# Hybrid decoder step on one core: the three partial products of a pair of k-tiles in another order

## The chip, the cores and the metric

One launch of the kernel runs on one NeuronCore of a Trainium2 chip. The metric is the device time of one execution in microseconds; the number given for a kernel is the median of several executions. All inputs and outputs lie in HBM. TensorE multiplies a stationary operand (the weights of a matmul, loaded by an instruction of its own, LDWEIGHTS) with a moving operand and adds the product into PSUM.

## The reference, cut to what matters

The layer takes 256 prompt tokens and 8 x 4 sample tokens, together 288 rows, through one decoder layer in float32. Nearly all of its arithmetic is products of these 288 rows with large weight matrices:

```
xn = rmsnorm(x, norm_mix)
z, xbc, dt, q, k, v, r, g, gate_a, gate_b = split(xn @ w_in)      # 2048 x 15408
branch_a = ssd(z, xbc, dt) @ w_ssd_out                            # 2048 x 2048
branch_b = gla(q, k, v, r, g) @ w_gla_out
h = x + (sigmoid(gate_a) * branch_a + sigmoid(gate_b) * branch_b) @ w_mix_out
h = h + cross_attend(rmsnorm(h) @ w_cq, mem_k, mem_v) @ w_co
up = causal_conv(rmsnorm(h) @ w_up)                               # 2048 x 11264
h = h + (silu(up[gate half]) * up[other half]) @ w_down           # 5632 x 2048
```

`mem_k` and `mem_v` of the prompt are `rmsnorm(mem) @ w_ck` and `@ w_cv`. The state updates of the convolutions, the SSD scan and the GLA scan are outputs too.

## The kernel before, in words

Every float32 operand of a projection is split into two halves, hi (the value rounded to the type in which TensorE takes it, `F32R`) and lo (the rest, rounded likewise). A product W·x is taken as three products, hi·hi, hi·lo and lo·hi, all added into the same PSUM accumulator.

The activations are kept transposed, channels on the 128 partitions and the 288 tokens in the free dimension, so a weight tile of 128 x 128 is the stationary operand and 128 x 288 of activations move. All projections but those of the memory go through `proj_w` (lines 114 to 138), called by `proj` with a matrix and a block of (mostly) 256 of its columns. It takes `nt` accumulators of 128 output channels (two for 256 columns; the narrow projection of `dt` has one), and walks down the contraction dimension:

- `wload` (lines 102 to 105) has SP's queue load four k-tiles of 128 x 256 into a tile `raw`, of which there are `RB` = 3.
- For each pair of k-tiles `wsplit` (lines 94 to 100) makes `whi` with a cast on ScalarE (line 97) and `wlo` = `raw` - `whi` with a subtraction on VectorE (line 99). There are `WB` = 5 buffers of each; a cast can be written only when the matmuls that read the buffer's former content are done.
- For each of the two accumulators j the six matmuls of the pair follow: line 129 is hi·hi and line 130 hi·lo, for k = 0 and then k = 1; line 133 is lo·hi for k = 0 and k = 1. So lines 129 and 130 load the same 128 x 128 weights one directly after the other. I call these six matmuls a group; two groups make a pair's twelve.
- After the last pair `cons` reads the accumulator. Four accumulators (`acc`) rotate.

The projections of the memory (`mem_proj`, lines 287 to 322) have the roles exchanged: activations are the stationary operand, 512 columns of weights move, and the order of lines 313, 314 and 317 is hi·hi, lo·hi for each of two accumulators, then hi·lo for both. They don't change. Nor do the small products of the attention, lines 1346 to 1348 and 1387 to 1389, which have the same three-product form.

`weave` runs the steps of a background part (the scans, the attention) between the steps of a projection. The framework orders the instructions of each engine when the program is built: it takes them in the order written where it holds their inputs for ready by then, and lets a later instruction pass where it doesn't. On the chip each engine's order is fixed and semaphores do the waiting. Matmuls that add into one accumulator keep their order.

Of the kernel before, what the change touches and what calls it, by code (L numbers as in the profile page):

```python
# [40 lines left out]
def hybrid_step(ctx: ExitStack, tc: tile.TileContext, I: dict, O: list):  # L41
# [3 lines left out]
    MM, TR = nc.tensor.matmul, nc.tensor.transpose  # L45
# [10 lines left out]
    def acc_tile():  # L56
        return ps.tile([P, 512], F32, tag="acc", bufs=4, name="acc")

    def mm_tile():
        return ps.tile([P, 512], F32, tag="mm", bufs=3, name="mm")  # L60
# [33 lines left out]
    def wsplit(raw):  # L94

        hi = wp.tile(list(raw.shape), F32R, tag="whi", bufs=WB, name="whi")
        S.copy(hi, raw)  # L97
        lo = wp.tile(list(raw.shape), F32R, tag="wlo", bufs=WB, name="wlo")
        V.tensor_tensor(lo, raw, hi, ALU.subtract)  # L99
        return hi, lo  # L100
# [8 lines left out]
    def flush():  # L109

        while late:
            late.pop(0)()

    def proj_w(load, ncol, X, nk, cons, N=T):

        nt = (ncol + P - 1) // P
        accs = [acc_tile() for _ in range(nt)]
        for k0 in range(0, nk, 4):
            kn = min(4, nk - k0)
            raw = load(k0, kn)  # L120
            for s0 in range(0, kn, 2):
                hi, lo = wsplit(raw[:, s0:s0 + 2, :])
                for j in range(nt):
                    m = min(P, ncol - j * P)
                    a = accs[j][0:m, 0:N]
                    cs = slice(j * P, j * P + m)
                    for k in range(2):
                        xh, xl = X(k0 + s0 + k)
                        MM(a, hi[:, k, cs], xh, start=(k0 + s0 + k == 0), stop=False)  # L129
                        MM(a, hi[:, k, cs], xl, start=False, stop=False)  # L130
                    for k in range(2):
                        xh, xl = X(k0 + s0 + k)
                        MM(a, lo[:, k, cs], xh, start=False, stop=(k0 + s0 + k == nk - 1))  # L133
                    if k0 + s0 + 2 == nk:
                        cons(j, a)
                if k0 + s0 == min(4, nk - 2):
                    flush()
                yield

    def proj(w, c0, ncol, X, nk, cons, row0=0):  # L140
        def load(k0, kn):
            return wload(w[row0 + k0 * P:row0 + (k0 + kn) * P, c0:c0 + ncol].rearrange("(k p) n -> p k n", p=P))
        return proj_w(load, ncol, X, nk, cons)
# [40 lines left out]
    def halves(alloc, name):  # L184

        ts = [alloc(f"{name}{i}") for i in range(2)]

        def at(k, n=None):
            t, o = ts[k // 8], k % 8
            if n is None:  # L190
                return t[:, o, :], t[:, 8 + o, :]
            return t[:, o:o + n, :], t[:, 8 + o:8 + o + n, :]
        return at
# [55 lines left out]
    X = halves(bigr, "xn")  # L249
    with pool("p0") as p0:  # L250
# [207 lines left out]
        def dt_cons(j, a):  # L458
# [4 lines left out]
            V.tensor_tensor(lr3[64:80, :], a[64:80], lr3[64:80, :], ALU.subtract)  # L463

        run(proj_w(dt_load, 112, X, KT, dt_cons))

        def dt_prep():
# [682 lines left out]
    for n in range(8):  # L1150
        kind, i = units[n]
# [66 lines left out]
    for j2 in range(KT // 2):  # L1218
        def cons(j, a, j2=j2):
            added(hx[j2][:, j, :], 2 * j2 + j, a, vec("norm_cross"), hn, acc)  # L1220
# [198 lines left out]
    a = mm_tile()  # L1419
# [143 lines left out]
    a = acc_tile()  # L1563
# [61 lines left out]
```

## Time and profile before

| | us |
|---|---|
| median of 3 runs (lowest to highest) | 2608.87 (2606.83 to 2610.24) |
| the profiled execution | 2607.92 |
| its span, first to last instruction | 2606.2 |
| TensorE matmul busy | 2576.2 (99%) |
| TensorE weight load busy | 2473.3 (95%) |
| VectorE, ScalarE, GpSimd busy | 1718.2, 1376.2, 308.2 |
| mean granted TensorE clock, as a share of full speed | 0.996 |

Weight loads stand in the profile on a row of their own (PEld) beside the matmuls (PE). Matmuls are pipelined: the duration of one covers parts of its neighbours, so the pace of a chain is read from the difference of the starts of successive matmuls. The profile names a matmul by its line, by the tiles it reads (`acc<-mx,whi`: activations `mx`, weights `whi`), and by the shapes of the stationary and the moving operand (128\*128, 128x288).

### The profile page before, as it was taken

To read this page: it belongs to the slowest core of one execution; us is meant where nothing else is said; L and a number is where in the kernel's file an instruction comes from. 1 tells how busy PE (TensorE), PEld (TensorE's weight loads), DVE (VectorE), ACT (ScalarE), POOL (GpSimd) and SP (SyncE) were. 2 spreads that over 40 slices of the span, in tenths; PEclk is the share of its full clock that TensorE was granted. 3 is DMA by queue.
4 is the path that set the end of the run, shared out by engine and by line. 5 is a ranking of instruction groups with operands and counts; after the bars stand their busy time and mean duration, and the time that the engine had idled before them with its cause. 6 is when DMAs were issued, how large, how long until landed. Compare 5 with 4: busy or idle time off the path is not lost. (4 is left out here: it accounts for less than half of the span.)

```text
span 2606.2 us, 50491 instructions
## 1 busy us (share of the span) xinstructions
PE 2576.2 (99%) x19123; PEld 2473.3 (95%) x19123; DVE 1718.2 (66%) x3683; ACT 1376.2 (53%) x2796; POOL 308.2 (12%) x425
## 2 busy tenths in 40 slices
PE   8999999999999999999999999999999999999998
PEld 7889999999989998999999989899999999999998
DVE  5655786886766566666666555567777677675765
ACT  7655655564645463534455544455545454454545
POOL 2003021100000000000000222202202020110200
PEclk9999999999999999999999999999999999999999
DMA  7666566665676666777666778655555555555553
GB/s 250 208 225 205 179 200 179 201 195 148 201 234 212 199 213 218 225 233 237 182 207 214 246 262 298 213 166 168 166 170 166 168 161 172 168 160 178 164 171 126
DMA packets 435280, 514.07 MB, mean 197 GB/s; under 512 B 23208, under 2 KB 384984, under 8 KB 434716
## 3 DMA queue, kind: packets, MB, share of 16 engines
q1 hardware_dynamic: 408684, 423.16, 52.5%
q0 software_dynamic: 26320, 87.68, 10.1%
q8 instruction: 150, 2.46, 0.4%
q14 instruction: 94, 0.77, 0.1%
q10 hardware_dynamic: 32, 0.01, 0.0%
HBM read 465.27 MB, written 45.48 MB: 196 GB/s over the span
## 5 line engine op out<-in xcount | busy, mean ns | idle before, releaser
L99 DVE TENSOR_TENSOR wlo<-raw,whi 128x512 fp32r<-128x512 f32 (+1 forms) x1464 | 989.5, 689 | 703.3 <-ACT whi L97 689.6
L97 ACT CAST whi<-raw 128x512 fp32r<-128x512 f32 (+1 forms) x1464 | 898.2, 618 | 1043.8 <-PE acc L130 824.1
L129 PE MATMUL acc<-xn,whi 128*128 128x288 f32 (+1 forms) x1936 | 551.0, 300 | 2.8 <-ACT whi L97 2.8
L130 PE MATMUL acc<-xn,whi 128*128 128x288 f32 (+1 forms) x1936 | 542.5, 295 | 0.0
L133 PE MATMUL acc<-xn,wlo 128*128 128x288 f32 (+1 forms) x1936 | 413.0, 295 | 1.4 <-DVE wlo L99 1.4
L129 PE MATMUL acc<-hf,whi 128*128 128x288 f32 x1408 | 396.0, 296 | 0.0
L130 PE MATMUL acc<-hf,whi 128*128 128x288 f32 x1408 | 393.5, 295 | 0.0
L129 PEld LDWEIGHTS acc<-xn,whi 128*128 128x128 f32 (+1 forms) x1936 | 365.0, 189 | 10.2 <-issue 6.7
L130 PEld LDWEIGHTS acc<-xn,whi 128*128 128x128 f32 (+1 forms) x1936 | 365.2, 189 | 4.2 <-issue 1.0
L133 PEld LDWEIGHTS acc<-xn,wlo 128*128 128x128 f32 (+1 forms) x1936 | 311.3, 188 | 1.8 <-DVE wlo L99 1.7
L133 PE MATMUL acc<-hf,wlo 128*128 128x288 f32 x1408 | 302.2, 296 | 0.0
L130 PEld LDWEIGHTS acc<-hf,whi 128*128 128x128 f32 x1408 | 265.1, 188 | 0.1
L129 PEld LDWEIGHTS acc<-hf,whi 128*128 128x128 f32 x1408 | 264.7, 188 | 0.1
L133 PEld LDWEIGHTS acc<-hf,wlo 128*128 128x128 f32 x1408 | 225.4, 188 | 0.0
L130 PE MATMUL acc<-pr,whi 128*128 128x288 f32 x704 | 196.6, 295 | 0.0
L129 PE MATMUL acc<-pr,whi 128*128 128x288 f32 x704 | 195.9, 294 | 0.0
L129 PE MATMUL acc<-un,whi 128*128 128x288 f32 x512 | 153.3, 315 | 2.3 <-DVE mb L897 1.0
L133 PE MATMUL acc<-pr,wlo 128*128 128x288 f32 x704 | 147.8, 291 | 0.0
L1457 POOL COPY fsp<-fst 128x16 f32<-128x16 f32 x88 | 105.4, 1222 | 335.3 <-ACT fcg L1463 87.8
L130 PE MATMUL acc<-un,whi 128*128 128x288 f32 x512 | 143.2, 295 | 0.0
L130 PEld LDWEIGHTS acc<-pr,whi 128*128 128x128 f32 x704 | 132.4, 188 | 0.0
L129 PEld LDWEIGHTS acc<-pr,whi 128*128 128x128 f32 x704 | 132.1, 188 | 0.0
(525 smaller groups left out, 4245.3 us busy)
## 6 DMA issues: line engine op xcount, KB each, us to landing
raw<-in_w_in_dram SPq DMA_DIRECT2D x240, 512.0 KB
raw<-in_w_up_dram SPq DMA_DIRECT2D x176, 512.0 KB
raw<-in_w_down_dram SPq DMA_DIRECT2D x88, 512.0 KB
raw<-in_w_ck_dram SPq DMA_DIRECT2D x32, 512.0 KB
raw<-in_w_cv_dram SPq DMA_DIRECT2D x32, 512.0 KB
raw<-in_w_ssd_out_dram SPq DMA_DIRECT2D x32, 512.0 KB
sin<-in_state_gla_dram POOLq DMA_DIRECT2D x32, 512.0 KB, 5.7
out_dram<-sin SPq DMA_DIRECT2D x32, 512.0 KB
```

Of the source, the lines that this page charges most:

```text
L97: S.copy(hi, raw)
L99: V.tensor_tensor(lo, raw, hi, ALU.subtract)
L129: MM(a, hi[:, k, cs], xh, start=(k0 + s0 + k == 0), stop=False)
L130: MM(a, hi[:, k, cs], xl, start=False, stop=False)
L133: MM(a, lo[:, k, cs], xh, start=False, stop=(k0 + s0 + k == nk - 1))
L1457: G.tensor_copy(sp[:, :, 0:2], st.rearrange("p (b k) -> p b k", k=2))
```

## The change

The six matmuls of a group are written in another order: first hi·hi for k = 0 and 1, then lo·hi for k = 0 and 1, then hi·lo for k = 0 and 1. In the weights they load, the order was hi0 hi0 hi1 hi1 lo0 lo1 and is hi0 hi1 lo0 lo1 hi0 hi1; in the activations they move, it was h0 l0 h1 l1 h0 h1 and is h0 h1 h0 h1 l0 l1. The start flag stays on the group's first matmul, and the stop flag is now on the last hi·lo. Nothing else changes: no instruction is added or taken away.

```diff
-                    for k in range(2):
-                        xh, xl = X(k0 + s0 + k)
-                        MM(a, hi[:, k, cs], xh, start=(k0 + s0 + k == 0), stop=False)
-                        MM(a, hi[:, k, cs], xl, start=False, stop=False)
-                    for k in range(2):
-                        xh, xl = X(k0 + s0 + k)
-                        MM(a, lo[:, k, cs], xh, start=False, stop=(k0 + s0 + k == nk - 1))
+                    xs_ = [X(k0 + s0 + k) for k in range(2)]
+                    for p, (wt, i) in enumerate(((hi, 0), (lo, 0), (hi, 1))):
+                        for k in range(2):
+                            MM(a, wt[:, k, cs], xs_[k][i], start=(k0 + s0 + k == 0 and p == 0),
+                               stop=(k0 + s0 + k == nk - 1 and p == 2))
```

## Rows read from the trace of the kernel before

**Rows 1.** Page: busy us (share of the span) and instructions of each engine.
```profile
PE 2576.2 (99%) x19123; PEld 2473.3 (95%) x19123; DVE 1718.2 (66%) x3683; ACT 1376.2 (53%) x2796; POOL 308.2 (12%) x425
```

**Rows 2.** Line 129 by tiles: count, duration ns min/median/max, first and last start us.
```profile
L129 PE MATMUL acc<-xn,whi x1936: 288/293/696, 112.9 to 1346.4; 128*128 128x288 f32 x192, 128*112 128x288 f32 x2
L129 PE MATMUL acc<-hf,whi x1408: 290/293/515, 1748.0 to 2487.6; 128*128 128x288 f32 x176
L129 PE MATMUL acc<-pr,whi x704: 290/292/378, 1901.8 to 2592.7; 128*128 128x288 f32 x176
L129 PE MATMUL acc<-un,whi x512: 290/293/696, 384.7 to 1245.3; 128*128 128x288 f32 x171
L129 PE MATMUL acc<-mx,whi x256: 290/293/293, 1346.9 to 1447.5; 128*128 128x288 f32 x128
L129 PE MATMUL acc<-hn,whi x256: 290/293/509, 1448.1 to 1618.7; 128*128 128x288 f32 x128
L129 PE MATMUL acc<-co,whi x256: 290/293/401, 1620.7 to 1747.5; 128*128 128x288 f32 x128
```

**Rows 3.** Timeline from 2000 us: start us, duration us, engine, line, tiles, count.
```profile
2000.59 0.30 PE L129 MATMUL acc<-hf,whi 128*128 128x288 f32 x1
2000.59 0.19 PEld L130 LDWEIGHTS acc<-hf,whi 128*128 128x128 f32 x1
2000.73 0.30 PE L130 MATMUL acc<-hf,whi 128*128 128x288 f32 x1
...
2003.81 0.30 PE L129 MATMUL acc<-hf,whi 128*128 128x288 f32 x1
```

**Rows 4.** Timeline of TensorE from 2040 us, the starts of two groups.
```profile
2040.15 0.29 PE L129 MATMUL acc<-pr,whi 128*128 128x288 f32 x1
...
2043.27 0.29 PE L129 MATMUL acc<-pr,whi 128*128 128x288 f32 x1
```

**Rows 5.** Timeline of TensorE from 190 us, in a memory projection (512 columns move).
```profile
189.96 0.39 PE L313 MATMUL acc<-whi,mn_hi 128*128 128x512 f32 x1
...
192.68 0.39 PE L313 MATMUL acc<-whi,mn_hi 128*128 128x512 f32 x1
```

**Rows 6.** Timeline of TensorE from 1517 us, in the attention (256 columns move).
```profile
1516.97 0.28 PE L1387 MATMUL mm<-pTh,vph 128*128 128x256 f32 x1
1517.09 0.28 PE L1388 MATMUL mm<-pTl,vph 128*128 128x256 f32 x1
1517.21 0.28 PE L1389 MATMUL mm<-pTh,vpl 128*128 128x256 f32 x1
...
1517.67 0.29 PE L129 MATMUL acc<-hn,whi 128*128 128x288 f32 x1
```

**Rows 7.** Timeline of TensorE from 326 us, in the scan (256 columns move).
```profile
325.99 0.40 PE L834 MATMUL mm<-bblk,wst 128*128 128x256 f32 x2
326.22 0.30 PE L129 MATMUL acc<-xn,whi 128*128 128x288 f32 x1
```

**Rows 8.** Busy time by stretch: matmuls, loads, DVE, ACT, POOL; clock, DMA share, GB/s.
```profile
1350.00:1440.00 90.00, 90.00 (x686) 90.00 (x685) 55.62 (x100) 45.26 (x86) 8.76 (x16) 1.00 0.69 227
```

**Rows 9.** Line 133, what TensorE sat idle for (us, times).
```profile
  DVE wlo L99: 3.1, 2
```

**Rows 10.** Line 129, the same.
```profile
  issue: 17.6, 51
  ACT whi L97: 10.9, 8
```

**Rows 11.** Line 130, the same.
```profile
  issue: 4.5, 19
```

**Rows 12.** Waits over the span: engine, line, releaser: total us, times, longest us.
```profile
ACT whi L97 <- PE acc L130: 824.1, 911, 3.2
DVE wlo L99 <- ACT whi L97: 689.6, 749, 9.6
```

**Rows 13.** Timelines of ScalarE and VectorE from 1400 us.
```profile
1402.23 0.62 ACT L97 CAST whi<-raw 128x512 fp32r<-128x512 f32 x1 [0.97 <-PE acc L130]
1403.80 0.62 ACT L97 CAST whi<-raw 128x512 fp32r<-128x512 f32 x1 [0.95 <-PE acc L130]
...
1402.89 0.69 DVE L99 TENSOR_TENSOR wlo<-raw,whi 128x512 fp32r<-128x512 f32 x1 [0.90 <-ACT whi L97]
```

**Rows 14.** Timeline of TensorE from 445.5 us, in a woven stage.
```profile
446.71 0.29 PE L130 MATMUL acc<-xn,whi 128*128 128x288 f32 x1
448.44 0.53 PE L133 MATMUL acc<-xn,wlo 128*128 128x288 f32 x2 [1.43 <-DVE wlo L99]
```

## The prediction

> **What bounds the kernel now.** I read the busy shares first: TensorE's matmuls are busy 99% of the span and VectorE, the next of the engines that compute, 66% [rows 1]. The same row tells that there are as many weight loads as matmuls, 19,123 each: a weight tile that two neighbours share is loaded twice all the same. Next the groups by line. Line 129 counts 1936 + 1408 + 704 + 512 + 3 x 256 = 5328 matmuls [rows 2]; lines 130 and 133 have as many by the code (two in each group of six), so the change touches 15,984 of the 19,123.
>
> Since matmuls overlap, their pace is read from starts. The cleanest stage is the projection with w_mix_out, where nothing is woven in: 256 matmuls of line 129 are 128 groups, and from the first of them (1346.9) to the last (1447.5, third of the last group) lie 127 x 6 + 2 = 764 matmuls in 100.6 us, 131.7 ns each [rows 2]. [...] 15,984 x 131.7 ns = 2105 us, 81% of the span. So nearly everything hangs on one number, the step from one projection matmul to the next, and a nanosecond on it is 16 us of the kernel.
>
> That step isn't quite constant. In one stretch of the up projection four groups, 24 matmuls, take 2003.81 - 2000.59 = 3.22 us, 134.2 ns each [rows 3]; in a down projection 24 take 3.12 us, 130.0 ns [rows 4]. Both are streams of the same written order and shapes in which nothing waits, so I take the step for a rhythm that the instruction stream falls into, not for a property of one line.
>
> Who waits for whom: ScalarE's cast waits 824.1 us in 911 waits for a `whi` buffer that line 130 still reads, and the subtraction waits 689.6 us for the cast [rows 12]. They are ahead of TensorE and held back by it. TensorE waits for `wlo` 3.1 us in two entries [rows 9], and at line 129 10.9 us in 8 for `whi` [rows 10]; both lists add the load's and the matmul's row.
>
> **The change, part by part.**
>
> *Loads.* None goes. Of the six steps of a group two went from a matmul to one with the same weights; none does afterwards. Does such a step cost differently? Within one group: line 129 starts at 2000.59, line 130, which reloads the same weights, at 2000.73, and its load started at 2000.59, with the matmul before it [rows 3]. So the load is hidden behind the earlier matmul even if the weights are equal. The attention shows the two kinds side by side with 256 columns: line 1387 to 1388 (same weights) 0.12 us, 1388 to 1389 (other weights) 0.12 us, and the six steps up to the next projection matmul 0.70 us, 116.7 ns each [rows 6]. I find no price on a shared weight tile.
>
> The trace has no 288-column stream without shared neighbours, so I bound its step. Two streams have none. With 512 columns the memory projections take 2.72 us for 12 matmuls, 226.7 ns [rows 5]. With 256 columns line 834, in other work, takes 0.23 us for 2, 115 ns [rows 7]. A straight line between these two at 288 columns is 115 + 32 x (226.7 - 115) / 256 = 129.0 ns; the same line from the attention's 116.7 ns gives 130.4. The upper bound is the slow rhythm, 134.2 ns [rows 3]. Ends: 129.0 (15,984 x -2.7 ns = -43 us) and 134.2 (15,984 x 2.5 ns = +40 us). I take 131.7, the stage that is the same kind of stream in the same shape, so 0 us.
>
> [...]
>
> *`wlo` is wanted earlier.* Before, four matmuls (0.53 us) stand between a pair's first hi matmul and its first lo matmul, now two (0.26 us). And the `whi` buffer is read until the pair's last matmul, two later than before, so the cast that waits for it starts 0.26 us later; `wlo` in turn comes free two matmuls earlier, which helps nobody, because its subtraction follows the cast. What was the cover? From the release, a cast at 1402.23 of 0.62 us and a subtraction at 1402.89 of 0.69 us are over after 1.35 us, and the next cast is 1.57 us behind the first [rows 13]. With five buffers the new pair's turn comes after the four that lie between, 4 x 1.58 = 6.3 us, plus 0.26 us that remained of its predecessor and 0.53 us of hi matmuls: 7.1 - 1.35 = 5.8 us of margin for `wlo`. Afterwards 6.3 + 0.26 - 1.35 = 5.2 us. Cost nothing where ScalarE and VectorE keep up, which is nearly everywhere; SP's loads of `raw`, three tiles ahead, shift by the same 0.26 us and are not nearer to the path. Where the cover is gone the pair loses up to 0.26 us: the two entries at `wlo`, one of them 1.43 us of idle [rows 14], and the eight at `whi`. Ten by 0.26 us is +2.6 us at most. Below nothing it can go only if the order of issue there happens to shift a background instruction better; nearest row, 1.43 us [rows 14]. I take +1 us. Behind a waiting TensorE stands everything that it issues, in order, so such a wait is paid in full.
>
> *The lo half of the activations is wanted later,* at the fifth matmul and not the second. It would pay where a projection starts on fresh activations, but line 130 has no wait for an activation in its list, only 4.5 us of "issue" in 19 [rows 11]. 0 us; the end below is those 4.5 us.
>
> *The order of issue.* In the woven stages the framework lets background instructions and the second accumulator's matmuls pass where it thinks that `wlo` is late. It will think so more often, and then has two hi matmuls of each accumulator to issue in between and not four. That moves scan instructions by fractions of a microsecond on an engine that is full: 0 us.
>
> *Sum.* 2607.92 (the profiled execution, 1.7 us over its span) + 0 + 1 + 0 + 0 = 2608.9, and the median of the runs shown is 0.95 us over that execution, so I write 2609. A difference of 0.2%, 5.2 us, is about what a measurement of this kernel can tell from none.
>
> **The rivals.**
>
> *The rhythm settles slower.* The new order could lock the stream onto the slow step more often. For it: the 134.2 ns exist [rows 3] in a stream where nothing waits. Against: nothing in the rows ties them to an order. All matmuls there would give 2609 + 40 = 2649, half of them 2629; it passes 0.2% when an eighth of the matmuls go from 131.7 to 134.2 ns (2000 x 2.5 ns = 5 us). Chance 0.25.
>
> *The rhythm settles faster.* The same with 130.0 ns [rows 4]: all of it 15,984 x -1.7 ns = -27 us, 2582; half 2595. It counts from a fifth of the matmuls on (3100 x 1.7 ns = 5.3 us). For it: the streams without shared neighbours at 256 and 512 columns point to 129.0 ns at 288. Against: line 834 runs two at a time in other work, so its 115 ns is a thin base. Chance 0.26.
>
> *`wlo` becomes the wait.* Slower: if the margin of 5.2 us were used up in the woven stages, at least 20 pairs would have to lose the full 0.26 us to make 5.2 us; 40 pairs give 2619. For it: one wait of 1.43 us stands there already [rows 14]. Against: it is the only one of note among 5328 / 4 = 1332 pairs. Chance 0.08.
>
> *The surplus goes.* The reloaded weights are what keeps the step above the columns' own time, through something that rows 6 are too few to show. Were half of the difference between 131.7 and a step of 0.43 ns per column (110 ns from 256 to 512 columns, rows 5 and 6; 288 x 0.43 = 124 ns) to go, that would be 15,984 x 3.9 ns = 62 us, 2547. Against: rows 5 and 6. Chance 0.02. [...]
>
> That the change does nothing because the framework puts the old order back is excluded within an accumulator, where matmuls keep their written order.
>
> **How the numbers follow.** No change in the step, 2609, own range 2604 to 2614: chance 0.39. Slower: 0.25 + 0.08, and of the likeliest case nothing: 0.33. Faster: 0.26 + 0.02 = 0.28. The range goes down to three quarters of the fast rhythm (-20 us) and up to somewhat over half of the slow one (+23 us): 2589 to 2632, which leaves out the extreme parts of the rhythm rivals and the last one, about 0.15 to 0.2.
>
> **What would show it.** Right: as many loads as before, 764 steps of the w_mix_out stage again in 100.6 us within 0.5, TensorE's waits for `wlo` still below 5 us, ScalarE still waiting some 800 us, now for the line that issues the last hi·lo. Wrong by rhythm: that stage or the up and down projections at another step with no new wait; each stage then differs by its own count times the difference. Wrong by waits: `wlo` at the head of TensorE's idle list, with tens of entries.

## The result, and the profile after

| | before | after |
|---|---|---|
| median us (runs) | 2608.24 (4) | 2620.14 (4), 2618.13 to 2623.94 |
| ratio to before, 95% interval | | 1.0047 [1.0029, 1.0064] |
| profiled execution, its span, us | 2607.92, 2606.2 | 2621.31, 2619.6 |

The changed kernel is slower by 0.3 to 0.6%, 12 us. Its page, busy us and instructions of each engine:

```profile
PE 2594.0 (99%) x19123; PEld 2492.0 (95%) x19123; DVE 1714.8 (65%) x3683; ACT 1373.8 (52%) x2796; POOL 251.0 (10%) x425
```

As many loads and matmuls as before, the same share, and 17.8 us more of matmul time than the 2576.2 us before [rows 1]. The span less that busy time went from 30.0 us to 25.6. So TensorE isn't waiting longer, its matmuls stand further apart. The waits of the changed kernel's matmuls (total us, times, longest us):

```profile
PE acc L311 <- ACT whi L97: 3.9, 2, 2.1
PE acc L130 <- DVE wlo L99: 3.3, 4, 2.0
PE acc L130 <- ACT whi L97: 2.1, 3, 1.4
```

and, from the list for line 130, which now issues all six matmuls of a group, what the load and the matmul rows sat idle for:

```profile
  issue: 19.7, 62
  ACT whi L97: 7.6, 11
  DVE wlo L99: 7.6, 8
```

`wlo` costs 7.6 us in 8 entries where it cost 3.1 in two [rows 9], `whi` 7.6 us where it cost 10.9, "issue" 19.7 where lines 129 and 130 had 17.6 and 4.5 [rows 10, 11]. That is 34.9 us now against 36.1, and with the smaller entries that the same lists show 41.2 us both times, so the waits have not grown.

The pace has. The stage of w_mix_out and two of its relatives (min/median/max of the duration in ns, first and last start):

```profile
L130 PE MATMUL acc<-mx,whi x512: 292/295/303, 1351.2 to 1453.4; 128*128 128x288 f32 x171
...
L130 PEld LDWEIGHTS acc<-hf,whi x2816: 186/188/193, 1753.3 to 2499.2; 128*128 128x128 f32 x188
L130 PEld LDWEIGHTS acc<-pr,whi x1408: 186/188/193, 1908.0 to 2606.3; 128*128 128x128 f32 x176
```

From the first matmul of 128 groups to the last one of the last group are 127 x 6 + 5 = 767 steps in 102.2 us: 133.2 ns (133.3 from the unrounded starts), against 131.7 [rows 2]. The granted clock was 1.00 from 1352 to 1453 us, no lower than in rows 8. TensorE's timeline in a down projection, where the step was 130.0 ns [rows 4]; matmuls of like tiles are merged, "x4" being the two hi·lo of one group and the two hi·hi of the next:

```profile
2059.89 0.69 PE L130 MATMUL acc<-pr,whi 128*128 128x288 f32 x4
2060.42 0.43 PE L130 MATMUL acc<-pr,wlo 128*128 128x288 f32 x2
...
2063.09 0.57 PE L130 MATMUL acc<-pr,whi 128*128 128x288 f32 x3
```

Four groups, 24 matmuls, take 3.20 us, 133.3 ns each, so two stages that stood at different paces before, w_mix_out at 131.7 and the down projection at 130.0, are alike now. I averaged all steps below 160 ns between two projection matmuls from the trace's starts: 131.90 ns before (15,329 steps), 132.99 after (15,363). 1.09 ns x 15,363 = 16.7 us. By stage, with the count of matmuls times the difference of the averages: w_mix_out 768 x 1.66 = 1.3 us; up projection 4224 x 0.50 = 2.1 (two fifths of its stretches of six matmuls stood at 806 or 807 ns before, the 134.2 ns of rows 3, and under 2% do now); down projection 2112 x 2.76 = 5.8; input and branch output projections 5808 x 1.05 + 1536 x 0.40 = 6.7; query and output 0.4 + 1.0. Together 17.3 us; the span grew by 13.4, and the 4.4 us by which TensorE's idle time fell are about the difference.

Inside the slow pace there is a pattern. In w_mix_out the successive steps after the change are 131, 131, 132, 140 ns and so on, in fours, and the load that goes with the long step takes 192 or 193 ns and not 187 or 188. Among the weight loads of the 15,984 matmuls that the change touches, 402 took 191 to 199 ns before and 3418 after, 2877 of them exactly four loads behind another such one.

### The profile page after: what moved, and what is told of

Its sections match the earlier page's. It is cut to its first block, busy times and chain, and to the rows that moved or that the text cites. A ratio compares the mean times of both kernels' runs of the same rounds, so it can differ in the third digit from the quotient of the medians.

```text
span 2619.6 us, 49909 instructions
## 1 busy us (share of the span) xinstructions
PE 2594.0 (99%) x19123; PEld 2492.0 (95%) x19123; DVE 1714.8 (65%) x3683; ACT 1373.8 (52%) x2796; POOL 251.0 (10%) x425
## 4 chain that ended last, share of the span: by engine, by line
PE 95%; DMA 2%; DVE 1%; ACT 0%; issue 0%; POOL 0%; DVEq 0%; ACTq 0%; POOLq 0%
PE acc L130 79%; PE acc L311 2%; PE acc L312 2%; PE acc L315 2%; PE mm L1266 1%; DMA raw<-in_w_in_dram 1%; PE la L1315 1%; PE mm L1084 1%; PE la L1378 1%; PE mm L1049 1%; PE mm L820 0%; PE la L1076 0%; DMA gw<-in_w_gla_gate_dram 0%; DVE wlo L99 0%; PE la L805 0%
## 5 line engine op out<-in xcount | busy, mean ns | idle before, releaser
L130 PE MATMUL acc<-xn,whi 128*128 128x288 f32 (+1 forms) x3872 | 714.4, 299 | 2.1 <-ACT whi L97 2.1
L130 PEld LDWEIGHTS acc<-xn,whi 128*128 128x128 f32 (+1 forms) x3872 | 582.9, 189 | 13.5 <-issue 7.4
L130 PE MATMUL acc<-hf,whi 128*128 128x288 f32 x2816 | 492.9, 297 | 0.0
L130 PEld LDWEIGHTS acc<-hf,whi 128*128 128x128 f32 x2816 | 415.3, 189 | 0.1
L130 PE MATMUL acc<-pr,whi 128*128 128x288 f32 x1408 | 248.1, 297 | 0.0
L130 PEld LDWEIGHTS acc<-un,whi 128*128 128x128 f32 x1024 | 153.9, 189 | 16.7 <-issue 9.8
L130 PEld LDWEIGHTS acc<-pr,wlo 128*128 128x128 f32 x704 | 113.5, 189 | 0.0
L130 PE MATMUL acc<-un,wlo 128*128 128x288 f32 x512 | 109.3, 295 | 0.0
L311 PE MATMUL acc<-whi,mn_hi 128*128 128x512 f32 x256 | 105.2, 411 | 3.9 <-ACT whi L97 3.9
L312 PE MATMUL acc<-whi,mn_lo 128*128 128x512 f32 x256 | 101.3, 396 | 0.0
```

What stands on the lines that cost most here:

```text
L130: MM(a, wt[:, k, cs], xs_[k][i], start=(k0 + s0 + k == 0 and p == 0), stop=(k0 + s0 + k == nk - 1 and p == 2))
L311: MM(accs[m], mn_hi[:, kk, ms_], hi[:, 0, :], start=(kk == 0), stop=False)
L312: MM(accs[m], mn_lo[:, kk, ms_], hi[:, 0, :], start=False, stop=False)
```

## The experiments

Time of each and ratio to the kernel before are from runs on the same chip. "Step" is the average of all steps below 160 ns, as above; "w_mix_out" the step in that stage alone; a count of slow loads is that of loads of 191 to 199 ns among the weight loads of the projections, 402 in the kernel before and 3418 after the change. In the diffs `seq` lists for each matmul the weights, their k, the k of the activations and their half (0 is hi, 1 is lo), and replaces the change's loop over the three products.

I began with theory S, that the missing shared neighbours (two matmuls in a row with the same weights) are the cause, since the change takes them away. Its rivals: W, the earlier `wlo` and later release; M, the order in which the activation tiles move, which the change permutes as well.

**No shared neighbours, but lo late**

```diff
+ seq = ((hi,0,0,0), (hi,1,1,0), (hi,0,0,1), (hi,1,1,1), (lo,0,0,0), (lo,1,1,0))
```

> Order of a group: hi0h0 hi1h1 hi0l0 hi1l1 lo0h0 lo1h1. No neighbours share weights, as after the change, but lo is wanted at the fifth matmul and the whi buffer comes free at the fourth, as before it. Theory S (steps onto the same weights keep the stream out of a slow pattern of four matmuls, so without them it falls into it): as after the change, about 2620 us, 133.3 ns a step in the w_mix_out stage, every fourth weight load of 192 ns and not 188. Rival W (lo wanted earlier and buffers freed later cost the time): as before, 2608 us. Rival M (the order in which the activation halves move sets the step): this order is a third one, so the step may be anything between 130.0 and 134.2 ns, 2580 to 2648 us, and equals that after the change only by chance.

Measured: 2622.27 us, ratio 1.0059 [1.0047, 1.0072], step 133.00, w_mix_out 133.3, 3338 slow loads. As slow as the change, though lo is wanted no earlier and the buffers come free no later than in the kernel before: W falls. TensorE's idle list has 7.4 us for `wlo` in 5 entries here, as much as the 7.6 us after the change, so the earlier lo isn't what raised that wait either.

**Shared neighbours, the halves swapped**

```diff
+ seq = ((hi,0,0,1), (hi,0,0,0), (hi,1,1,1), (hi,1,1,0), (lo,0,0,0), (lo,1,1,0))
```

> Order of a group: hi0l0 hi0h0 hi1l1 hi1h1 lo0h0 lo1h1. The weights follow one another as before the change (two shared steps in six), the activations move in another order. Theory S: as before, 2604 to 2613 us, steps of 130 to 132 ns in the w_mix_out stage, few loads over 191 ns. Rival M: unlike before, anything from 2580 to 2648 us. Rival W: as before, 2608 us.

Measured: 2608.12 us, 1.0003 [0.9992, 1.0014], step 131.91, w_mix_out 131.7, 396 slow loads. As before in every stage, to 0.11 ns. S has it right, and M in its simple form not; but the swap exchanges only hi and lo of one k-tile.

**One shared neighbour**

```diff
+ seq = ((hi,0,0,0), (hi,0,0,1), (hi,1,1,0), (lo,0,0,0), (lo,1,1,0), (hi,1,1,1))
```

> Order of a group: hi0h0 hi0l0 hi1h1 lo0h0 lo1h1 hi1l1. One shared step in six where there were two before and none after. Theory S: between the two, some 2614 us, 132.5 ns a step, the pattern of four broken once in six steps. Rival W: lo wanted at the fourth matmul, buffers freed at the sixth: 2614 us too, but with TensorE's idle time for wlo as the difference and the step at 131.7 ns. Rival M: anything between 130.0 and 134.2 ns.

Measured: 2605.91 us, 0.9998 [0.9989, 1.0006], step 131.95. Not between the two, but as before: half of the shared steps are gone at no cost. By stage it is not the kernel before: the down projection steps at 131.8 ns and not 130.5, the up projection at 132.0 and not 132.8, and the two nearly cancel. The first doubt about S.

**All weights the same**

```diff
+ seq = ((hi,0,0,0), (hi,0,0,1), (hi,0,1,0), (hi,0,1,1), (hi,0,0,0), (hi,0,1,0))
```

> Every matmul of a group loads the weights hi of k = 0; the activations move as before the change (h0 l0 h1 l1 h0 h1), the numbers of instructions are the same. hi of k = 1 and both lo tiles are made but take no part, so the products aren't those of the reference. Five steps in six are onto the same weights. Theory S, if each shared step saves the same: from 133.3 (none) to 131.7 (two in six) is 4.8 ns per shared step, so 133.3 - 5/6 x 4.8 = 129.3 ns, about 2608 - 38 = 2570 us. Theory S, if sharing only breaks the pattern of four: between 130 and 132 ns, 2580 to 2613 us. Rival M: the same moving order as before, 131.7 ns, 2608 us.

Measured: 2601.78 us, 0.9977 [0.9968, 0.9986], step 131.78, w_mix_out 131.7, 382 slow loads. In w_mix_out it is the pattern of the kernel before, with five shared steps in six where that has two. By their place in the group the six steps of that stage average 131.2, 131.9, 129.2, 132.4, 133.0 and 132.5 ns in the kernel before, and 131.2, 132.5, 129.0, 132.2, 133.3 and 131.8 ns here. The first and the third are the shared ones of the kernel before; they are the short ones here too, where all are shared within the group. So a shared step has no price of its own. (Of the 5 us by which this run is ahead, 0.12 ns a step makes 2; the rest I can't place.) That left "sharing breaks the pattern" against M, and the next two separate weights from activations.

**The weights' order of after with the activations' order of before, and equal weights with the activations' order of after**

```diff
+ seq = ((hi,0,0,0), (hi,1,0,1), (lo,0,1,0), (lo,1,1,1), (hi,0,0,0), (hi,1,1,0))   # first
+ seq = ((hi,0,0,0), (hi,0,1,0), (hi,0,0,0), (hi,0,1,0), (hi,0,0,1), (hi,0,1,1))   # second
```

> The weights follow one another as after the change (hi0 hi1 lo0 lo1 hi0 hi1), the activations move as before it (h0 l0 h1 l1 h0 h1). The pairs that this makes aren't the three products, so what is computed isn't the reference. Theory S (sharing weights with the neighbour is what matters): as after, 133.3 ns a step in the w_mix_out stage, every fourth load of 192 ns, 2620 us. Theory M (the order in which the activation tiles move): as before, 131.7 ns and 2607 us.

> Every matmul of a group loads hi of k = 0, the activations move as after the change (h0 h1 h0 h1 l0 l1). hi of k = 1 and both lo tiles take no part, so what is computed isn't the reference. Theory S: five shared steps in six, as in the run with the same weights and the moving order of before, 131.7 ns and 2602 us. Theory M: as after, 133.3 ns with a load of 192 ns in every fourth place, 2615 to 2620 us.

Measured: the first 2600.6 us, 0.9981 [0.9972, 0.9990], step 131.75; the second 2617.85 us, 1.0047 [1.0030, 1.0064], step 132.97. Their w_mix_out rows, 767 steps from first to last, first the one with no shared neighbours:

```profile
L130 PE MATMUL acc<-mx,whi x512: 292/294/297, 1342.5 to 1443.5; 128*128 128x288 f32 x171
```

and the one whose neighbours nearly all share:

```profile
L130 PE MATMUL acc<-mx,whi x768: 292/294/302, 1347.2 to 1449.5; 128*128 128x288 f32 x192
```

101.0 us, 131.7 ns, against 102.3 us, 133.4 ns. With the activations' order of before the stage steps at 131.7 ns under three sets of weights, with that of after at 133.3 under two. The order of the activations decides; S is refuted by both runs. The weights of before with the activations of after were not run.

**The products of one k-tile together**

```diff
+ seq = ((hi,0,0,0), (lo,0,0,0), (hi,0,0,1), (hi,1,1,0), (lo,1,1,0), (hi,1,1,1))
```

> Order of a group: hi0h0 lo0h0 hi0l0 hi1h1 lo1h1 hi1l1, the three products of one k-tile and then those of the other. No neighbours share weights. Theory S: as after, 133.3 ns and 2620 us. Theory M, if what hurts is that the two k-tiles' activations alternate from matmul to matmul: they change only once in three steps, so no pattern of four, between 130.0 and 132.5 ns, 2585 to 2615 us.

Measured: 2623.59 us, 1.0069 [1.0056, 1.0081], step 133.17, and only 315 slow loads. My guess that alternation as such hurts was wrong: this order changes the k-tile once in three matmuls and is the slowest, at a flat 133.3 ns:

```profile
1399.79 0.29 PE L130 MATMUL acc<-mx,wlo 128*128 128x288 f32 x1
...
1401.39 0.29 PE L130 MATMUL acc<-mx,wlo 128*128 128x288 f32 x1
```

Twelve matmuls (every third is a lo one, four of these apart) in 1.60 us.

**The order of after, halves side by side.** What about an activation tile can matter if not which values it holds? Its place. In a tile of activations the k-tiles stand 1152 bytes apart, which is an odd multiple of 128; hi and lo of a k-tile are 9216 bytes apart, a multiple of 256. So k = 0 and k = 1 start 128 bytes apart modulo 256, and hi and lo of one k-tile start alike. Theory A is M by address; its rival is the logical order. The edit puts hi and lo of a k-tile side by side (the next line, for slices of several k-tiles, is changed likewise and left out here).

```diff
-                return t[:, o, :], t[:, 8 + o, :]
+                return t[:, 2 * o, :], t[:, 2 * o + 1, :]
```

> The changed kernel with its order, but the activation tiles of the up, mix, query, output and input projections lie in SBUF in another place: hi and lo of a k-tile side by side and not eight tiles apart. So k and k + 1 of one half are 2 x 1152 bytes apart, and its two halves 1152. Theory A (M by address: a step hurts when the moving tile's start changes by an odd multiple of 1152 bytes each time): the moving starts now change once in four or two steps, no pattern of four in these stages, w_mix_out at 130 to 132 ns, and 2605 to 2614 us. Theory M by logical order: as after, 133.3 ns, 2620 us. Theory S: as after, too.

Measured: 2612.21 us, 1.0022 [1.0012, 1.0031], step 132.32. The same instructions in the same order, tiles elsewhere, and about half of the loss is gone, though w_mix_out at 132.2 ns is just above the 130 to 132 that I had expected. In the same run `pr`, whose layout I left, keeps the slow pace. Its timelines in an up and then a down projection:

```profile
2000.02 0.69 PE L130 MATMUL acc<-hf,whi 128*128 128x288 f32 x4
...
2003.19 0.43 PE L130 MATMUL acc<-hf,whi 128*128 128x288 f32 x2
...
2058.88 0.43 PE L130 MATMUL acc<-pr,wlo 128*128 128x288 f32 x2
...
2062.08 0.43 PE L130 MATMUL acc<-pr,wlo 128*128 128x288 f32 x2
```

24 matmuls each: 3.17 us, 132.1 ns, for `hf`; 3.20 us, 133.3 ns, for `pr`.

**Two other orders with the halves side by side**

The same edit on the kernel before, and on the order by k-tile:

> The kernel before with its order, hi and lo of a k-tile side by side in xn, mx, hn, co and hf (pr and un as they were). Modulo 256 bytes the moving starts of a group now go 0 1 0 1 0 0 and not 0 0 1 1 0 1, still four changes in six steps. Theory A: another rhythm than before in these five stages, between 130 and 132.5 ns, and pr as before at 130.5 ns; 2585 to 2615 us. Rival O: the same steps as before in all stages, 131.7 ns in w_mix_out, 2607 us.

> The order by k-tile (hi0h0 lo0h0 hi0l0 hi1h1 lo1h1 hi1l1), hi and lo of a k-tile side by side in xn, mx, hn, co and hf. Modulo 256 bytes the moving starts of a group go 0 0 1 0 0 1, a period of three. Theory A: no longer the flat 133.3 ns of this order in these five stages, between 129.5 and 132.5 ns, while pr keeps 133.3; 2590 to 2612 us. Rival O: 133.3 ns everywhere, 2623 us, as the same order had with the halves apart.

Measured: 2610.45 us, 1.0017 [1.0008, 1.0026], w_mix_out 132.2 (131.7 with the halves apart), `pr` 131.6 and not 130.5; and 2617.7 us, 1.0044 [1.0032, 1.0057], w_mix_out 132.2 (133.3 apart), `pr` 133.3. The layout moved w_mix_out in both, up in the one and down in the other. Two misses: by k-tile I expected under 132.5 ns in all five stages and at most 2612 us, and `xn` and `hn` stayed at 133.1; and `pr` of the first left its 130.5 though neither its order nor its layout changed. So order and layout don't fix the pace alone; what else it depends on no run here shows.

**All tiles alike.** With k-tiles 1280 bytes apart, 5 x 256, all starts differ by multiples of 256. The room is paid with one buffer of `whi` and `wlo`, so the totals carry waits of their own; the steps are what counts.

```diff
-WB = 5
+WB = 4
-        return big.tile([P, KT, T], F32R, tag="bigr", bufs=2, name=name)
+        return big.tile([P, KT, 320], F32R, tag="bigr", bufs=2, name=name)[:, :, 0:T]
```

> The kernel before with its order, but the activation tiles of the input, query and up projections (xn, hn, hf) stand 1280 bytes apart and not 1152, 32 unused columns behind each; to make room there are 4 buffers of whi and wlo and not 5. mx, co, pr and un keep 1152. Theory A (by address: what counts is how the moving tiles' starts follow one another modulo 256 bytes; 1152 is 4 x 256 + 128, 1280 is 5 x 256, so now all starts are alike): the order has nothing to act on, and the step in xn, hn and hf is that of rare changes, 133.3 ns, no load of 192 ns in every fourth place; 5808 x 1.6 + 768 x 1.3 + 4224 x 0.5 ns = about +13 us, 2619 us, and a few us more if four buffers are too few; mx and pr as before, 131.7 and 130.5 ns. Rival O (the logical order of halves and k-tiles counts, wherever they lie): as before in all stages, 2607 us and what four buffers cost.

> The changed kernel with its order, the activation tiles of the input, query and up projections (xn, hn, hf) 1280 bytes apart and not 1152, and 4 buffers of whi and wlo, as in the run of the kernel before with that pitch. Theory A: where all moving starts are alike modulo 256 bytes the order has nothing to act on, so xn, hn and hf step at 131.7 ns, as they did there with the order of before, and show no load of 192 ns in every fourth place, while pr and mx, whose tiles stand 1152 apart, keep the 133.3 ns of the changed kernel. By these steps 768 x 1.7 + 768 x 1.3 + 1536 x 0.4 + 2112 x 1.5 ns = 6 us over the run with the order of before, 2630 us, and up to 10 us more where lo two matmuls earlier finds four buffers too few. Rival O (the logical order counts): xn and hf at 132.8 and 133.3 ns as in the changed kernel, 13 us more, 2643 us or over.

Measured, order of before: 2624.47 us, 1.0066 [1.0043, 1.0088]. Its step in `xn` is 131.71 ns, `hn` 131.70, `hf` 131.67; I had expected 133.3, so I had the pace of like starts wrong; and `pr`, which I had expected to keep its 130.5, stands at 131.7. Order of after: 2636.34 us, 1.0106 [1.0086, 1.0125], `xn` 131.69, `hn` 131.76, `hf` 131.67, and where the pitch stayed 1152, w_mix_out 133.3 and `pr` 133.1. In the up projection, before's order and then after's, 24 matmuls in 3.16 us both times:

```profile
1999.71 0.29 PE L129 MATMUL acc<-hf,whi 128*128 128x288 f32 x1
...
2002.87 0.29 PE L129 MATMUL acc<-hf,whi 128*128 128x288 f32 x1
```

```profile
1999.79 0.69 PE L130 MATMUL acc<-hf,whi 128*128 128x288 f32 x4
...
2002.95 0.69 PE L130 MATMUL acc<-hf,whi 128*128 128x288 f32 x4
...
2058.92 0.42 PE L130 MATMUL acc<-pr,wlo 128*128 128x288 f32 x2
...
2060.52 0.42 PE L130 MATMUL acc<-pr,wlo 128*128 128x288 f32 x2
```

The last two rows are 12 matmuls of a down projection with after's order: 1.60 us, 133.3 ns. Where all tiles start alike, the two orders step alike to 0.06 ns; where they don't, in the same executions, they differ: w_mix_out by 1.65 ns as in the result, `pr` by 1.4. That is the change's cost switched off and left on within one run. The pattern inside a group goes with it: by place in the group the steps of `hf` average 131.0 to 134.1 ns in the kernel before and 131.2 to 135.4 after the change, and with the pitch of 1280 bytes 131.5 to 131.9 in both orders. Why the totals are higher all the same, what TensorE sat idle for at lines 133 and 129 in the first run (before's order), to be held against rows 9 and 10:

```profile
  DVE wlo L99: 18.5, 20
  ACT whi L97: 21.0, 13
```

and at line 130 in the second:

```profile
  DVE wlo L99: 30.1, 41
  ACT whi L97: 15.0, 10
```

Span less busy time of TensorE is 42.9 and 46.3 us, against 30.0 before. So four buffers are too few here, and with the order of after more so.

**All runs with five buffers.** 0 and 1 stand for the two places of a moving tile's start modulo 256 bytes, relative to each other, in `xn`, `mx`, `hn`, `co` and `hf`:

| order and layout | starts in a group | step ns | w_mix_out ns | us |
|---|---|---|---|---|
| after's weights, before's activations | 0 0 1 1 0 1 | 131.75 | 131.7 | 2600.6 |
| all hi0, before's activations | 0 0 1 1 0 1 | 131.78 | 131.7 | 2601.8 |
| before | 0 0 1 1 0 1 | 131.90 | 131.7 | 2608.2 |
| halves swapped | 0 0 1 1 0 1 | 131.91 | 131.7 | 2608.1 |
| one shared | 0 0 1 0 1 1 | 131.95 | 131.7 | 2605.9 |
| before, interleaved | 0 1 0 1 0 0 | 132.16 | 132.2 | 2610.5 |
| after, interleaved | 0 0 0 0 1 1 | 132.32 | 132.2 | 2612.2 |
| by k, interleaved | 0 0 1 0 0 1 | 132.83 | 132.2 | 2617.7 |
| all hi0, after's activations | 0 1 0 1 0 1 | 132.97 | 133.3 | 2617.9 |
| after | 0 1 0 1 0 1 | 132.99 | 133.3 | 2620.1 |
| none shared, lo late | 0 1 0 1 0 1 | 133.00 | 133.3 | 2622.3 |
| by k | 0 0 0 1 1 1 | 133.17 | 133.3 | 2623.6 |

Rows with the same sequence of starts agree in w_mix_out to the digit shown, whatever their weights are. In other stages they need not: by k, interleaved, `xn` stands at 133.1 and w_mix_out at 132.2. The times come from several chips, on which the kernel before alone took 2605.1 to 2608.5 us, so rows that are that close aren't ordered by them. The first row and the last are from one chip: 23.0 us for 1.42 ns, 16.2 us per ns, where 15,984 matmuls make 16.0. No version beats both kernels by more than the noise and computes the layer; the two fastest rows leave products out.

## Why the prediction was right or wrong

*The time* lay in the range, on its slower half: 12 us over before, where the likeliest case said no change and gave itself 2604 to 2614. That the range held is in part luck: its upper end was made from a pace of 134.2 ns, which is not what came.

*The step of a projection matmul* is the term that failed. The prediction asked only whether a step onto the same weights has a price, found none, and took "131.7, the stage that is the same kind of stream in the same shape, so 0 us". The finding holds: with all weights the same the pace of the kernel before returns in w_mix_out. The conclusion doesn't, because the change also permutes the activations, and no term of the sum priced that. It measured +1.09 ns a step, 16.7 us, inside the bounds of 129.0 to 134.2 ns. The trace of the kernel before had a hint that rows 6 did not: in w_mix_out the shared steps average 130.2 ns and the others 132.4. Whoever had priced that as sharing would have forecast 0.76 ns x 15,984 = 12 us, the measured time from the wrong cause, since with all weights the same these places stay short. "Nothing in the rows ties them to an order" was right of the rows, but I read the two paces of rows 3 and 4 as states between which an order might shift the shares; instead the order brought a pace that stood in neither, 133.3.

*The line through 512 and 256 columns* (129.0 ns without shared neighbours) pointed the wrong way: without them w_mix_out stands at 131.7 or 133.3 ns, by the order of the activations. The streams of rows 5 and 7 move other tiles, from other places; whether that is the reason I did not test.

*The rival "the rhythm settles slower"* had the sign and the place: no new wait, each stage off by its own count. Its mechanism was not what came: the 134.2 ns onto which it had the stream lock is nearly gone from the up projection, and the new pace is 133.3. So its price, all matmuls at 134.2 ns, was too high.

*`wlo` earlier*: +1 us taken, 2.6 at most. Its entries went from 3.1 to 7.6 us, those of `whi` from 10.9 to 7.6; the sum of the waits didn't rise. The order with lo late was not faster (2622.27 us) and has 7.4 us for `wlo`, so the earlier lo cost nothing that can be seen.

*Lo activations later, order of issue*: 0 taken, and TensorE's idle time fell by 4.4 us; I didn't separate what gave that.

*The surplus*: the rival that the reload makes it fell. Half of the way from 131.7 ns to the 124 ns that it had estimated from rows 5 and 6 would have been 127.8 ns; w_mix_out stood at 131.7 to 133.3 ns in every run, with shared neighbours and without.

*What the prediction told to look at* did show it: w_mix_out at another step with no new wait is what it had named "wrong by rhythm". Of its signs for "right", the waits for `wlo` below 5 us failed as well (7.6 us), and ScalarE's wait for the line that issues the last hi·lo came near its 800 us (900.0 us in 954).

## What to carry to other kernels

When TensorE is full, read the step from the starts of a clean stage, and before reordering matmuls list everything that the order permutes: the weights, the moving tiles, and where these lie. A change that touches two operands at once needs crossings (the new weights with the old activations, and the other way round or with the weights all equal) before its own description is believed. And a nanosecond in a step is worth a look only if it is multiplied by the count: here 16 us.

## What the runs showed of the hardware that I had not expected

The pace of back-to-back matmuls with 288 float32 columns depended here on where the moving tiles start relative to one another, through the order in which they come: 131.7 ns in `xn`, `hn` and `hf` if all start alike modulo 256 bytes (pitch 1280) in both orders, and 131.7, 132.2 or 133.3 ns in w_mix_out with a pitch of 1152, according to the sequence. Which weights were loaded, and whether two neighbours loaded the same, made no difference there: one sequence of starts (0 0 1 1 0 1) gave 131.7 ns and another (0 1 0 1 0 1) 133.3 ns, each under three sets of weights. Only these two pitches were run: that starts count modulo 256 bytes fits w_mix_out in every row of the table but rests on one layout of like starts, and what in the chip does it stays open.

One order and layout also had several paces: the kernel before ran its up projections at about 131.7 ns and at 134.2, and its down projections mostly at 130.0, with the same sequence of starts. What selects among them is open too.
